# Five of seven Strassen products of the first two units as four-byte matmuls, and what moves with them

## The chip, the cores and the metric

One NeuronCore of a Trainium2 chip. The metric is the time of one execution on the device in microseconds (us). TensorE multiplies matrices, VectorE and ScalarE work element by element, GpSimd (POOL) does small things and issues the stores, SyncE (SP) issues the loads.

## The reference

A trunk of two layers, 2048 prompt tokens and 8 x 8 sample tokens, 1024 channels, all float32:

```python
h = rms_norm(x, pre_g)
z = jnp.einsum("btd,de->bte", h, w_in)          # 1024 -> 6 * 512
...
o = jnp.einsum("bte,ed->btd", jnp.concatenate([ya, yb], axis=-1), w_out)
return x + rms_norm(o, post_g), new_a, new_b
```

In the first layer (even) the mixers are a gated convolution of 3 taps (A) and a causal pooling with windows 2, 4, 8, 16 whose result goes through a 128 x 128 matrix per group (B). In the second (odd) they are a spatial gating within chunks of 128 tokens (C) and a convolution of 31 taps with a layer norm (D).

## The kernel before, in words

The work has six phases. Phases 0 and 1 are the input projection of layer 0 for the prompt's first and second 1024 tokens (a segment), phase 2 its output projection; phases 3 to 5 are the same for layer 1. A phase of input projection has 12 units. A unit multiplies 256 output channels by 1024 tokens, as one Strassen step in Winograd's form: seven products instead of eight, each of 4 tiles over the contraction (`KH` = 4), 128 x 128 by 128 x 512. Weights are the stationary side (A), activations the moving one (B). To reach float32 accuracy with matmuls in the reduced four-byte type `float32r`, each operand is split into a rounded high part (a cast on ScalarE) and a low part (a subtraction on VectorE), and each tile takes three matmuls: low by high, high by low, high by high (`mms`, L931 to L937). The activations' parts are `Bh` and `Bl`, split by `b_split` (L671); the weights' are `ahi` and `alo`, by `a_unit` (L477) and `lo_job` (L449). The sums of weight quarters (`comb`, L540) and of activation quarters (L829) that Strassen needs are made by VectorE too. Phase 0 writes its weights' sums and their low parts to DRAM (`wsd`, `wld`), and phase 1 loads them from there (L405 to L423).

The product order is `ORDER` (L44); for the first two units, which run as a pair, it is `FIRST` (L45). A pair (`TWINS`, L63) takes turns by product: unit 0's product j, unit 1's product j, so that what a product needs has twice the time. Pairs are units 0 and 1 and units 10 and 11 of phase 0, and units 10 and 11 of phase 3. The last unit of a phase frees one activation buffer after the other, and the next phase's activations are loaded (`b_proc`, L679) and split into them.

`start_proc` (L746) prepares phase 0. It loads the transposed prompt in two halves of 512 tokens, squares it (ScalarE) and adds the squares (VectorE, L762), sums over partitions with TensorE (L767), takes the mean and the root (L773 to L776), spreads the result over the partitions with four diagonal tiles `dg` and TensorE (L778 to L784), normalises 16 tiles in place (L744) and forms the sums. `h1_proc` (L837) does this for the second segment, stores the sums in DRAM (`td`, L702 to L709), and only then do the loads of phase 1's activations find all they need. `smp_states` (L1103) loads a state of the samples at the beginning of phase 1 and copies it with ScalarE. `pool_mix` (L1148) is mixer B's matrix. In the output projections, `unit_z` (L1066) leaves two PSUM banks per 128 tokens, and `post` (L1955) normalises them with VectorE, adds the residual and, in layer 0, transposes the result for phase 3.

The order of all instructions is found while the program is built, by a planner (`Plan`, L79): processes yield what they wait for (a condition, a time, VectorE time), and at each step of TensorE's planned time the first process that is ready goes on, in order of priority, 0 first. VectorE is filled at most 1 us ahead of TensorE. Each engine then runs its queue in that order. On-chip buffers are 36 slots shared by three classes, `U` (results), `Wp` (weights) and `R` (loads); `KEEP` (L34) reserves some per phase.

## Time and profile before

| | us |
|---|---|
| median of 3 runs | 1560.34 |
| lowest, highest | 1555.58, 1560.35 |
| the profiled execution | 1556.43 |
| its span, first to last instruction | 1554.7 |
| TensorE busy | 1479.5 (95%) |
| VectorE busy | 1100.3 (71%) |
| ScalarE busy | 768.1 (49%) |
| mean granted clock of TensorE | 0.981 |

The profile is of one execution. Matmuls are pipelined, so a matmul's recorded time is longer than the distance from its start to the next one's; the distance is its cost in a stream. A four-byte (unsplit) matmul is recorded as two instructions.

### The profile page before, as it was taken

How to read it: one execution, taken by the hardware profiler on the slowest of the kernel's cores; microseconds unless marked ns; L12 is line 12 of the kernel's file. 1: busy time of each engine (PE TensorE's matmuls, PEld its weight loads, DVE VectorE, ACT ScalarE, POOL GpSimd, SP SyncE). 2: the span in 40 equal slices, each digit the busy share in tenths (PEclk: the TensorE clock that was granted, in tenths of full speed). 3: DMA queues.
4: the chain of work that ended last, by engine and by line, in shares of the span. 5: the costliest groups of instructions: out<-in, count | busy, mean ns of one | idle time of the engine just before them, and what ended most of it. 6: DMA issues, size and time to landing. Idle time of an engine off the chain costs nothing. (4 is left out here: it accounts for less than half of the span.)

```text
span 1554.7 us, 22198 instructions
## 1 busy us (share of the span) xinstructions
PE 1479.5 (95%) x6762; PEld 1200.7 (77%) x6762; DVE 1100.3 (71%) x1853; ACT 768.1 (49%) x1606; POOL 439.9 (28%) x841
## 2 busy tenths in 40 slices
PE   5699999799999999999979999989999999899997
PEld 4588887688888888878857888868888878788775
DVE  6977787675656557667663798978578988885532
ACT  5555434464554454445455655555544455724411
POOL 1243433112121105665643311000120023234421
PEclk9799999999999999999989999989999999999999
DMA  4466777989788878899999899998557688947641
GB/s 171 161 214 228 276 251 272 318 271 329 267 315 271 281 235 264 288 308 345 346 359 347 272 323 355 331 337 273 176 164 220 196 264 275 306 153 224 200 147 61
DMA packets 230297, 403.92 MB, mean 260 GB/s; under 512 B 28450, under 2 KB 77874, under 8 KB 230179
## 3 DMA queue, kind: packets, MB, share of 16 engines
q1 hardware_dynamic: 190466, 274.09, 54.1%
q0 software_dynamic: 39712, 128.43, 22.0%
q8 instruction: 53, 0.87, 0.2%
q14 instruction: 66, 0.53, 0.1%
HBM read 272.96 MB, written 129.45 MB: 259 GB/s over the span
## 5 line engine op out<-in xcount | busy, mean ns | idle before, releaser
L935 PE MATMUL bank_b<-Bh,alo 128*128 128x512 f32 (+1 forms) x848 | 342.3, 404 | 21.8 <-DVE alo L452 11.3
L935 PE MATMUL bank_b<-Bl,ahi 128*128 128x512 f32 (+1 forms) x848 | 337.2, 398 | 4.0 <-ACT ahi L285 4.0
L935 PE MATMUL bank_b<-Bh,ahi 128*128 128x512 f32 (+1 forms) x848 | 336.5, 397 | 0.0
L285 ACT CAST ahi<-araw 128x512 fp32r<-128x512 f32 (+1 forms) x404 | 238.4, 617 | 23.0 <-DMA araw<-yd 6.1
L935 PE MATMUL bank_a<-Bh,alo 128*128 128x512 f32 (+1 forms) x496 | 202.0, 407 | 5.4 <-DVE o L1972 3.3
L935 PEld LDWEIGHTS bank_b<-Bh,alo 128*128 128x128 f32 (+1 forms) x848 | 160.2, 189 | 59.9 <-ACT ahi L285 9.9
L935 PE MATMUL bank_a<-Bl,ahi 128*128 128x512 f32 (+1 forms) x496 | 198.3, 400 | 6.0 <-ACT ahi L285 4.8
L935 PE MATMUL bank_c<-Bh,alo 128*128 128x512 f32 (+1 forms) x496 | 198.9, 401 | 2.1 <-ACT Bh L285 2.0
L935 PE MATMUL bank_c<-Bl,ahi 128*128 128x512 f32 (+1 forms) x496 | 196.8, 397 | 4.0 <-ACT ahi L285 2.8
L935 PE MATMUL bank_a<-Bh,ahi 128*128 128x512 f32 (+1 forms) x496 | 197.0, 397 | 0.0
L935 PE MATMUL bank_c<-Bh,ahi 128*128 128x512 f32 (+1 forms) x496 | 196.3, 396 | 0.0
L935 PEld LDWEIGHTS bank_b<-Bl,ahi 128*128 128x128 f32 (+1 forms) x848 | 160.5, 189 | 40.8 <-ACT ahi L285 4.9
L935 PEld LDWEIGHTS bank_b<-Bh,ahi 128*128 128x128 f32 (+1 forms) x848 | 160.2, 189 | 39.2
L452 DVE TENSOR_TENSOR alo<-araw,ahi 128x512 fp32r<-128x512 f32 (+1 forms) x164 | 108.3, 681 | 74.3 <-ACT ahi L285 72.7
L935 PEld LDWEIGHTS bank_a<-Bl,ahi 128*128 128x128 f32 (+1 forms) x496 | 94.2, 190 | 27.7 <-ACT ahi L285 6.2
L935 PEld LDWEIGHTS bank_a<-Bh,alo 128*128 128x128 f32 (+1 forms) x496 | 94.1, 190 | 25.8 <-DVE o L1972 3.7
L935 PEld LDWEIGHTS bank_c<-Bl,ahi 128*128 128x128 f32 (+1 forms) x496 | 93.5, 188 | 25.4 <-ACT ahi L285 4.0
L935 PEld LDWEIGHTS bank_a<-Bh,ahi 128*128 128x128 f32 (+1 forms) x496 | 93.9, 189 | 22.5
L935 PEld LDWEIGHTS bank_c<-Bh,alo 128*128 128x128 f32 (+1 forms) x496 | 93.2, 188 | 23.2 <-ACT Bh L285 2.4
L935 PEld LDWEIGHTS bank_c<-Bh,ahi 128*128 128x128 f32 (+1 forms) x496 | 93.3, 188 | 22.5
L1487 DVE SCALAR_TENSOR_TENSOR fc<-fs,wsum,fc 128x512 f32<-128x512 f32 x120 | 90.1, 751 | 3.4
L675 DVE TENSOR_TENSOR Bl<-braw,Bh 128x512 fp32r<-128x512 f32 x116 | 74.5, 686 | 24.9 <-ACT Bh L285 24.7
(283 smaller groups left out, 2426.1 us busy)
## 6 DMA issues: line engine op xcount, KB each, us to landing
araw<-wx SPq DMA_DIRECT2D x144, 256.0 KB
araw<-wsd SPq DMA_DIRECT2D x144, 256.0 KB
alo<-wld SPq DMA_DIRECT2D x144, 256.0 KB
alo<-wlx SPq DMA_DIRECT2D x96, 256.0 KB
praw<-wi SPq DMA_DIRECT2D x72, 256.0 KB
araw<-yd SPq DMA_DIRECT2D x64, 256.0 KB
araw<-wi SPq DMA_DIRECT2D x48, 256.0 KB
wld<-alo POOLq DMA_DIRECT2D x48, 256.0 KB, 3.8
```

What stands on the lines that cost most here:

```text
L285: nc.scalar.copy(out=out, in_=in_)
L452: nc.vector.tensor_tensor(out=lo, in0=x, in1=hi.bitcast(F32), op=SUB)
L675: nc.vector.tensor_tensor(out=Bl[j][:, k, :], in0=r, in1=Bh[j][:, k, :].bitcast(F32), op=SUB)
L935: nc.tensor.matmul(out=out[:m], lhsT=w[k][:, :m], rhs=r[:, k, :], start=(start and k == 0 and w is l), stop=(stop and k == KH - 1 and w is ...
L1487: nc.vector.scalar_tensor_tensor(out=C, in0=sm[:, j:j + HM], scalar=w, in1=C, op0=MUL, op1=ADD if j else SUB)
```

## The change

Units 0 and 1 of phase 0 compute products 0, 3, 1, 5, 2 (`PLAIN`, in that order) with unsplit operands, one four-byte matmul per tile (`mms_plain`), products 4 and 6 as before. `a_first` makes their weights, `start_proc` orders norms, sums and splits anew; all 28 activation tiles are still split, for the later units. Low parts of weight sums 1, 2 and 5 of these units are not stored; phase 1 makes them itself (`no_low`). Units 10 and 11 of phase 0 are no pair any more. `h1_proc` and the posts of `unit_z` go to priority 1. The last output unit of phase 2 copies its banks to slots. Mixer B's matrix takes one four-byte matmul in segment 0 and for the samples. The output states are stored later.

```diff
-KEEP = ((18, 14), (12, 16), (16, 10), (14, 12), (18, 10), (12, 10))
+KEEP = ((22, 10), (12, 16), (16, 10), (14, 12), (18, 10), (12, 10))
-FIRST = (0, 3, 1, 2, 4, 5, 6)
+FIRST = (0, 3, 1, 5, 2, 4, 6)
+
+PLAIN = (0, 3, 1, 5, 2)
-TWINS = ((0, 0), (0, 10), (3, 10))
+TWINS = ((0, 0), (3, 10))
...
+    def no_low(lay, i, j):
+
+        return lay == 0 and (j in XT or i < 2 and j in PLAIN)
...
-                        lo, _ = load(kind, wld[lay][i, SIDX[j]], "alo", F32R)
+                        lo = None if no_low(lay, i, j) else load(kind, wld[lay][i, SIDX[j]], "alo", F32R)[0]
...
-                               and (u > 1 or st["x"] >= 3) and (kind == "w" or y_tile_ready(lay, key, i)))
+                               and (u > 1 or st["x"] >= 3) and (u != 2 or (1, 2) in prod) and (kind == "w" or y_tile_ready(lay, key, i)))
...
+    def a_first(u):
...
+        def later(j, n=1):
+            yield ("c", lambda: (u, j) in prod)
+            Wp.free(n)
+        sat = {}
+        yield from fetch(0)
+        plain(0, x[0])
+        yield from fetch(3)
+        plain(3, x[3])
+        yield from fetch(1)
+        yield from fetch(2)
+        yield ("c", Wp.room)
+        S = Wp.take([P, 512], "asum")
+        yield from comb(1, S, x[1], x[2], ADD)
+        plain(1, S)
+        yield from comb(4, x[1], x[0], x[1], SUB)
+        yield ("c", lambda: (u, 0) in prod)
+        yield ("u", sat[1])
+        yield from comb(2, x[0], S, x[0], SUB)
+        plain(2, x[0])
+        pl.spawn(later(1), 2)
+        yield ("c", lambda: (u, 3) in prod)
+        yield from comb(5, x[3], x[3], x[0], SUB)
+        plain(5, x[3])
+        pl.spawn(later(2), 2)
+        pl.spawn(later(5), 2)
+        yield ("c", lambda: all((e, 1) in prod for e in range(2)))
+        yield from split(4, x[1], pl.dve)
+        yield from split(6, x[2], pl.pe)
...
-            at = act(out=s4, in_=ps, dep=pl.pe)
+            nc.vector.tensor_scalar(out=s4, in0=ps, scalar1=1.0 / DM, scalar2=EPS, op0=MUL, op1=ADD)
...
-                dg = sp.tile([P, P], F32, tag="dg", name="dg", bufs=2)
+                dg = dgs[:, i * P:(i + 1) * P]
...
-            pl.spawn(by_columns(c), 1)
+            pl.spawn(by_columns(c), 0)
...
+        yield ("c", lambda: len(prog[0]) == 4)
+        yield ("t", 0.3)
+        yield from norm(0, range(KD))
+        aux_free()
+        yield ("c", lambda: len(prog[1]) == 4)
+        yield ("t", 0.3)
+        for k in range(KH):
+            split(0, k, (0, k))
+        yield from norm(1, range(KH))
+        yield ("c", lambda: (0, 1) in made and (1, 1) in made)
+        yield ("c", both(0))
+        yield from sums(1, (0, 0), (1, 0), (0, 0), 0)
+        yield from norm(1, range(KH, KD))
+        aux_free()
+        yield ("c", lambda: (0, 5) in made and (1, 5) in made)
+        yield ("c", both(1))
+        yield from sums(2, (0, 0), (1, 1), (0, 0), 1)
+        yield from sums(4, (1, 0), (1, 1), (1, 0))
+        for k in range(KH):
+            pl.spawn(drop(4, k, lambda: True), 1)
+            split(3, k, (0, k + KH))
+        yield ("c", both(3))
+        yield from sums(6, (0, 1), (0, 1), (0, 0), 3)
+        for k in range(KH):
+            split(5, k, (1, k + KH))
...
+    def mms_plain(out, ph, u, j, start):
+        t, = a_need(u, j)
+        w = f4(t[0])
+        for k in range(KH):
+            if (j, k) not in plain_ok:
+                pl.drain(lambda: (j, k) in plain_ok)
+            nc.tensor.matmul(out=out, lhsT=w[:, k, :], rhs=plain_x[j, k], start=(start and k == 0), stop=(k == KH - 1),
+                             skip_group_check=True)
+            pl.tick(0.92)
+        del ready[u, j]
+        prod.add((u, j))
...
+            if u + 1 == phase_units[2][1]:
+
+                t = U.take([P, 512], "o")
+                act(out=t[:m], in_=bk[:m])
+                done_bank(key)
+                bk, key = t, None
...
-        pl.spawn(go(), 2)
+        pl.spawn(go(), 1)
...
+        if whole:
+            w = cst[:, C_PW + cb * P:C_PW + (cb + 1) * P]
+            nc.tensor.matmul(out=ps[:, :n], lhsT=w, rhs=dd, start=True, stop=True)
+            pl.pe += 0.92
...
-                yield from pool_mix(cb, dd[:, 0:CH], CH, self.sg[c], dd[:, 0:CH], dh, dl)
+                yield from pool_mix(cb, dd[:, 0:CH], CH, self.sg[c], dd[:, 0:CH], self.s == 0)
...
-        yield ("c", lambda: all(y_ready(0, b, NPR, NSAMP) for b in range(KD)) and U.room())
+        yield ("c", lambda: all(y_ready(0, b, NPR, NSAMP) and y_ready(0, b, SEG + CH, CH) for b in range(KD)) and U.room())
...
-        pl.spawn(h1_proc(), 3)
+        pl.spawn(h1_proc(), 1)
```

## Rows read from the trace of the kernel before

**Rows 1.** The page, busy us by engine, and TensorE's busy tenths in 40 slices.

```profile
PE 1479.5 (95%) x6762; PEld 1200.7 (77%) x6762; DVE 1100.3 (71%) x1853; ACT 768.1 (49%) x1606; POOL 439.9 (28%) x841
...
PE   5699999799999999999979999989999999899997
```

**Rows 2.** Busy us (instructions) in stretches; then PEclk, DMA share, GB/s.

```profile
20.00:27.20 7.20, 3.99 (x16) 3.62 (x17) 5.71 (x11) 3.07 (x8) 1.26 (x2) 1.00 0.01 2
27.20:63.40 36.20, 22.46 (x74) 16.07 (x73) 36.13 (x61) 19.29 (x35) 4.48 (x8) 0.83 0.12 44
63.40:88.20 24.80, 24.75 (x98) 19.99 (x99) 17.07 (x29) 12.52 (x23) 7.62 (x16) 0.90 0.79 276
88.20:236.00 147.80, 147.80 (x645) 119.82 (x644) 115.84 (x200) 70.32 (x150) 60.87 (x113) 1.00 0.71 246
```

**Rows 3.** Waits of TensorE: us in total, times, longest.

```profile
PE bank_b L935 <- DVE alo L452: 11.3, 2, 9.5
...
PE bank_b L935 <- ACT bank_b L285: 8.0, 1, 8.0
```

**Rows 4.** Timeline of TensorE in units 0 and 1: start, us, instruction.

```profile
27.24 0.77 PE L935 MATMUL bank_a<-Bh,alo 128*128 128x512 f32 x1
...
38.15 0.40 PE L935 MATMUL bank_a<-Bh,ahi 128*128 128x512 f32 x1
38.38 0.39 PE L935 MATMUL bank_a<-Bh,alo 128*128 128x512 f32 x1
...
46.79 0.63 PE L935 MATMUL bank_c<-Bh,alo 128*128 128x512 f32 x1
47.21 0.63 PE L935 MATMUL bank_c<-Bl,ahi 128*128 128x512 f32 x1
...
63.45 0.77 PE L935 MATMUL bank_b<-Bh,alo 128*128 128x512 f32 x1 [9.50 <-DVE alo L452]
...
88.34 0.40 PE L935 MATMUL bank_a<-Bh,alo 128*128 128x512 f32 x1
```

**Rows 5.** Groups of VectorE from 20 to 67 us: count, busy us, mean ns.

```profile
L675 DVE TENSOR_TENSOR Bl<-xT,Bh 128x512 fp32r<-128x512 f32 x24 | 14.9, 681 | 0.2 <-ACT Bh L285 0.2
L744 DVE SCALAR_TENSOR_TENSOR xT<-xT,cst,rb 128x512 f32<-128x512 f32 x16 | 11.0, 740 | 0.0
L829 DVE TENSOR_TENSOR xT<-xT 128x512 f32<-128x512 f32 x16 | 9.9, 680 | 0.0
```

**Rows 6.** Timeline of TensorE, the gating product in phase 3.

```profile
857.78 1.05 PE L1629 MATMUL sg<-wmb,v 128*128 128x128 f32 x8
```

**Rows 7.** Timeline of ScalarE and of VectorE at the start.

```profile
17.04 0.40 ACT L781 ACTIVATE dg<-ident,r 128x128 f32<-128x128 f32 x1 [1.20 <-PE rb L784]
...
21.60 0.74 DVE L744 SCALAR_TENSOR_TENSOR xT<-xT,cst,rb 128x512 f32<-128x512 f32 x1
```

**Rows 8.** Timeline of TensorE in units 10 and 11 of phase 0.

```profile
262.72 0.53 PE L935 MATMUL bank<-Bh,alo 128*128 128x512 f32 x1 [2.46 <-DVE alo L452]
```

**Rows 9.** Timeline of VectorE and of SyncE's queue before phase 1.

```profile
285.80 0.68 DVE L707 TENSOR_TENSOR xT<-xT,xT 128x512 f32<-128x512 f32 x1
...
290.13 0.32 SPq L691 DMA_DIRECT2D braw<-td  x1
```

**Rows 10.** Phase 1's first unit: timeline of ScalarE, then stretches as in rows 2.

```profile
306.29 0.75 ACT L285 COPY smp<-stmp 128x64 f32<-128x64 f32 x2 [7.37 <-DMA stmp<-sab]
...
309.01 0.57 ACT L285 COPY bank_b<-bank_a 128x512 f32<-128x512 f32 x1
...
301.60:309.60 8.00, 0.00 (x0) 0.00 (x0) 2.02 (x4) 3.31 (x8) 0.00 (x0) 0.65 1.05 389
309.60:315.00 5.40, 5.36 (x14) 4.26 (x15) 5.17 (x10) 3.84 (x8) 0.00 (x0) 0.57 0.76 262
```

**Rows 11.** Phase 2 to phase 3: timeline of TensorE, then the stretch.

```profile
791.76 0.80 PE L935 MATMUL bank_a<-Bh,alo 128*128 128x512 f32 x1 [3.31 <-DVE o L1972]
...
783.00:791.80 8.80, 2.52 (x11) 1.47 (x9) 7.76 (x13) 7.85 (x16) 7.03 (x8) 0.63 1.03 378
```

More of the change, by code (lines that the diff above doesn't have):

```diff
@@ L447, in trunk, with fetch, plain, comb @@
     made = set()
+    prod, plain_ok = set(), set()
+    def a_first(u):
+        i = seq[u][3]
+        x = {}
+        def fetch(q):
+            yield ("c", lambda: (u, q) in raws)
+            x[q], at = raws.pop((u, q))
+            yield ("u", at)
+        def plain(j, t):
+            ready[u, j] = (t,)
+            made.add((u, j))
+        def comb(j, out, p, q, op):
+            yield ("d", tt_cost(512))
+            nc.vector.tensor_tensor(out=out, in0=p, in1=q, op=op)
+            sat[j] = store(wsd[0][i, SIDX[j]], out, lambda: s_ok[0].add((i, j)))
+        def split(j, t, at):
+            yield ("c", lambda: Wp.room(2))
+            hi = Wp.take([P, 512], "ahi", F32R)
+            lo = Wp.take([P, 512], "alo", F32R)
+            at = act(out=hi, in_=t, dep=at)
+            def after():
+                if j in SIDX:
+                    store(wld[0][i, SIDX[j]], lo.bitcast(F32), lambda: l_ok[0].add((i, j)))
+                Wp.free()
+            pl.spawn(lo_job(t, hi, lo, at, (u, j), after), 0)
+        def later(j, n=1):
[26 more added lines that the diff above has]
+        yield from split(6, x[2], pl.pe)
     def lo_job(x, hi, lo, at, key, after):
@@ L786, in by_columns, with both, drop, have @@
             yield ("t", 1.2)
+            R.free()
             prog[c].extend(range(4))
         def split(j, kk, key):
-            pl.spawn(b_split(0, j, kk, x[key], pl.dve + 0.12, U.free if j in (4, 5, 6) else lambda: None), 1)
+            pl.spawn(b_split(0, j, kk, x[key], pl.dve + 0.12, lambda: None), 1)
+        def both(*js):
+            return lambda: all((e, j) in prod for e in range(2) for j in js)
+        def drop(j, kk, more):
+            yield ("c", lambda: (j, kk) in bready[0] and more())
+            U.free()
+        def have(j, kk, key):
+            plain_x[j, kk] = x[key]
+            plain_ok.add((j, kk))
         def columns(c):
@@ L818, in start_proc @@
             for k in range(KH):
                 def key(cq):
[L820 to L827 removed]
+                    return cq[0], cq[1] * KH + k
@@ L1019, in bank_take, with fin12 @@
                 take_bank(key[k])
+        def fin12():
+            bank_free("c")
+            con.c12_done()
         for j in combos(u):
-            hl = parts(u, j)
-            b_wait(ph, j)
+            plain = u < 2 and j in PLAIN
+            if not plain:
+                hl = parts(u, j)
+                b_wait(ph, j)
             if j in (0, 1):
@@ L1964, in post @@
         for h in range(2):
-            o.append(U.take([P, 512], "o"))
+            o.append(U.take([P, 512], "o") if banks[h][1] is not None else banks[h][0])
         gpost, gpre = rows["gpost"], rows.get("gpre")
```

109 lines of the change are left out of this document (56 added, 53 removed).

## The prediction, made before the run

> **What bounds the kernel now.** I read the page's busy line and 40 slices first. TensorE is busy for 1479.5 of 1554.7 us [rows 1], so at most 75 us of idle time can be won, plus what is lost at half clock. The slices say where: the first two, hardly any in the middle. Next I cut the start into stretches [rows 2]. From 27.2 to 63.4 us TensorE works 22.46 of 36.2 us, while VectorE is busy 36.13 of 36.2 us with 61 instructions, 0.59 us each: there **VectorE sets the pace**. From 88.2 to 236 us TensorE has no idle time at all, and VectorE 116 of 148. So what is won at the start must be won in units 0 and 1. The waits of TensorE [rows 3] name the rest: 11.3 us for a low part of the weights (9.5 of it in one wait) and 8.0 us for one copy of a bank, elsewhere.
>
> The timeline of TensorE [rows 4] gives prices. The pair of units begins at 27.24 us, unit 2 at 88.34: 61.1 us. Split matmuls of 512 columns stand 0.23 us apart at full clock (38.15, 38.38) and 0.42 to 0.43 at 1.2 GHz (46.79, 47.21). The pair has 2 x 7 x 4 x 3 = 168 of them, 39.0 us at 0.232; so 22 us go to waits and half clock. What VectorE does meanwhile [rows 5]: 24 low parts of the activations, 16 normalisations, 16 sums. The low parts stand ahead of the weights' sums in its queue: the matmul at 63.45 waited 9.50 us.
>
> **The change, part by part.**
>
> *Matmuls.* 2 x 5 x 4 = 40 groups of three split matmuls become one four-byte matmul each. The nearest row is the gating product: eight recorded instructions, four four-byte matmuls of 128 columns, 1.05 us from the first start to the last end [rows 6]. Each of the eight lasts some 0.27 us, so the starts stand (1.05 - 0.27) / 7 = 0.111 us apart, and 4 x 128 = 512 columns take 8 x 0.111 = 0.89 us. Three split ones take 0.70. So TensorE gets 40 x 0.19 = 7.7 us more work, and the pair needs 40 x 0.89 + 16 x 0.70 = 46.7 us. The bounds: 0.70 (no dearer) and 1.05 (the row whole); I take 0.89. The Trainium skill, page "FP8 and Floating Point Precision", section "TensorE Precision Notes", has true FP32 take four passes through the array. By that rule a matmul costs 4 x 0.23 = 0.93 us and the pair 48.3; the trace agrees within 5%.
>
> *The start.* Four diagonal tiles take a slot each in one buffer, where two took turns: ScalarE's second waited 1.20 us for TensorE [rows 7], and with it the squares of the second half. The mean is taken by VectorE straight from PSUM, no copy. I take 1 us per half. The first normalisation began at 21.60 us [rows 7], and a plain product needs nothing but that: first matmul at 22 us, not 27.24. If the planner leaves the second half's statistics ahead of it on TensorE, as now, it is 25.5.
>
> *The pair.* 22 + 46.7 + 2.5 (half clock: 0.90 of 24.8 us in the second stretch [rows 2], as one warm-up) + 3 (the statistics matmuls between; TensorE was busy 3.99 us with such from 20 to 27.2 [rows 2]) + 2 for stalls = **76**. Is VectorE in time? Until the fifth product's operands exist it must do 16 normalisations, 8 sums of activations, 8 of weights and 8 low parts: 40 x 0.6 = 24 us from 20.4, so 44.5, while TensorE comes to that product at 22 + 5.5 + 4 x 7.1 = 56. Products 4 and 6 need 24 more, the leftover splits 8 more and the banks' sums 6: 23 us, so 67, against 69 for product 6. Close; hence the 2 us. Gain: 88.3 - 76.2 = **12 us**, between 88.3 - 71.2 = 17 (no stall, no statistics between) and 88.3 - 84 = 4 (late first matmul, 6 us of stalls). The cover is VectorE's remaining queue: if it runs late, unit 2 waits instead, since its tiles are now fetched only after unit 1's product 2.
>
> *What is moved off.* Ten casts and ten subtractions fewer here, 10 x 0.6 = 6 us of VectorE (in the sum above already), and six stores of low parts on GpSimd's queue. Phase 1 loads six tiles fewer on SyncE's queue, but makes these six low parts itself: 3.6 us of VectorE where activations are being split too.
>
> *Twin (0, 10) gone, h1 at priority 1.* These go together. The pair cost a wait of 2.46 us at 262.72 [rows 8], and it was there to spread phase 1's 28 activation splits over two units. But the sums for phase 1 ended at 285.80 us, and SyncE issued the load that needs them at 290.13 [rows 9]: the splits could not spread anyway. With h1 earlier they can begin at unit 11, with 19.5 us for 28 x 0.6 = 16.8 us of VectorE; behind each wait there stand the low parts of unit 12's weights. I cost that at a new stall of 2.5 us against 2.5 saved: 0, bounds +4 and -6.
>
> *The copy of the samples' state.* Late loads filled the DMA queues (1.05 from 301.6 to 309.6 us), ScalarE stood 7.37 us before the copy of the state, behind it the bank's copy, and TensorE 8.0 us [rows 3, 10]; then 0.57 of the clock for 5.4 us costs 2.3 more [rows 10]. The wait on that DMA stays in the code; what goes is the crowd of loads ahead of it. I take 7 of 10.3, bounds 0 and 10.3.
>
> *Last output unit of phase 2.* Its banks are copied by ScalarE (two copies, 0.57 us each as the bank's copies) and freed; phase 3 waited 3.31 us for VectorE's reading of one, and TensorE worked 2.52 of 8.8 us there [rows 11], 6.3 idle, with 0.63 of the clock. ScalarE is at 7.85 of 8.8 us and the DMA at 1.03 there, so the next weights come late. I take 5, bounds 0 and 8.8. Posts at priority 1 go with this.
>
> *Pooling.* Eight products of the first segment whole: 8 x 0.19 = +1.5 us of TensorE; eight casts and subtractions less, hidden. The samples' four, the later state store and KEEP: 0, beside a busy TensorE; bounds +1 and -1.
>
> Sum: 12 + 0 + 7 + 5 - 1.5 = 22.5 us off the profiled execution's 1556.4 (span 1554.7): 1533.9. The median of the runs is 1560.34, 3.9 above; two of three lie there, one at 1555.58. I add half of that: **1536**.
>
> **The rivals.**
>
> *Only the pair pays.* A new plan puts new stalls at the boundaries for the old: for it, the DMA at 1.03 to 1.05 in both [rows 10, 11]. 12 - 1.5 = 10.5: 1546, so 1548 as a median. Chance 0.22.
>
> *The debt is paid in units 2 to 5.* VectorE has 32 us free of 148 there [rows 2], yet h1 at priority 1 goes ahead of the weights' low parts, and product splits are left over; 10 us of waits come where none are. 1557, chance 0.10.
>
> *Turns: slower.* The sums are written in place over tiles that plain matmuls read, so VectorE's queue waits for TensorE, and TensorE then for the 8 instructions behind: 4.8 us at three changes of product, 14.4, and 2.5 of half clock after each, 7.5. The pair would end at 98, 9.8 later than now, the pooling adds 1.5, and the boundaries, whose work hangs on that queue, stay: 1567.7, so 1570 as a median. Against it: product 3 lies between 0 and 1, and 5 between 1 and 2, 7.1 us of cover for 4.8. It decides if unit 2 starts after 88.3. Chance 0.09.
>
> *TensorE the bound.* If the waits of the pair were hidden, only dearer matmuls would be left: 7.7 + 1.5, so 1566 and 1568 as a median. For it speaks 95% busy, against it the 13.7 us idle of 36.2 [rows 2]. The four-pass rule above speaks for this. Chance 0.03.
>
> **How the numbers follow.** Forecast 0.56. A difference under 0.3%, 4.7 us, can't be told from none. Faster: 0.56 + 0.22 + 0.02 of the debt's case, 0.80; same 0.08; slower 0.09 + 0.03 = 0.12. Low end: 17 + 4 + 10.3 + 8.8 off 1556.4, 1516. High end: past the second case and the debt's, 1558. That leaves out the slower cases and little else. The forecast's own range is 1516 to 1546.
>
> **What would show it.** Right: plain matmuls, two recorded each, 0.89 us a pair of records, the first at 22 us, unit 2 at 74 to 78; phase 1 begins near 280 with no wait of 7 us before the state's copy; a product of phase 3 straight behind the last output unit. Wrong: VectorE idle before sums with TensorE as the releaser (turns), waits of units 2 to 5 for low parts (debt), or a full DMA and the same gaps at both boundaries.

## The result, and the profile after

The changed kernel takes **1544.38 us** (median of 5 runs, 1539.90 to 1547.83), the kernel before 1560.34 in the 5 runs beside them. The ratio is **0.9902, 95% interval 0.9872 to 0.9931**: faster by about 1%, some 16 us. The profiled execution took 1544.38 us, its span is 1542.7 us, so 12.0 shorter than the span of before that the prediction was summed against. The forecast had 22.5 there.

The page first: busy times by engine, then TensorE's busy tenths.

```profile
PE 1482.0 (96%) x6710; PEld 1186.9 (77%) x6710; DVE 1090.5 (71%) x1839; ACT 758.6 (49%) x1584; POOL 439.7 (29%) x833
...
PE   6999999999999999999989999988999999899997
```

Against [rows 1] TensorE's busy time hardly moved (the plain matmuls are dearer), its first slices filled (5 6 9 9 to 6 9 9 9 in short), and nothing of the middle tells where 10 us went missing. For that the two traces have to be laid side by side. The same instructions are looked up in both, and the difference of their starts is the gain so far. The samples' matmuls (`zs`, one group after product 0 and one after product 6 of each unit) mark phases 1 and 4; the squares of the posts (`junk`, 34 of them) mark phase 2.

```
                                    before   after    gain so far
unit 2, first matmul                  88.3     76.1      12.2
phase 1, group 1 of the samples      297.7    284.3      13.4
phase 1, group 2                     326.5    306.9      19.6
phase 1, group 4                     350.8    334.8      16.0
phase 2, first squares               579.8    563.5      16.3
phase 2, last squares                785.4    774.5      10.9
phase 3, first transpose (vt)        839.5    827.0      12.5
phase 4, group 25                   1060.8   1042.5      18.3
phase 4, group 26                   1079.5   1067.0      12.5
last split matmul                   1546.3   1534.4      11.9
```

Up to phase 2 the gain is 16.3 us, where the forecast's terms for that stretch (12 + 0 + 7 - 1.5) make 17.5. From there on the forecast added 5 more; the kernel lost 4.4. **So the first half of the forecast came nearly as worked out, and the second half is where it fell short.** Both traces are single executions, and what that means for the second half shows only in the experiments.

*The pair.* TensorE's timeline (start, us, instruction; two records are one four-byte matmul):

```profile
19.68 2.08 PE L1049 MATMUL bank_a<-xT,araw 128*128 128x512 f32 x2 [1.82 <-DVE xT L813]
...
23.11 5.47 PE L1049 MATMUL bank_a<-xT,araw 128*128 128x512 f32 x6
28.37 1.24 PE L857 MATMUL rb<-dgs,ones 128*128 128x128 f32 x8
...
32.88 3.60 PE L1049 MATMUL bank_a<-xT,araw 128*128 128x512 f32 x8
36.32 3.60 PE L1049 MATMUL bank<-xT,araw 128*128 128x512 f32 x8
...
67.73 0.50 PE L1039 MATMUL bank_b<-Bl,ahi 128*128 128x512 f32 x1 [1.40 <-DVE Bl L744]
...
69.92 0.79 PE L1039 MATMUL bank_b<-Bl,ahi 128*128 128x512 f32 x1 [1.23 <-DVE Bl L744]
...
76.11 0.40 PE L1039 MATMUL bank_a<-Bh,alo 128*128 128x512 f32 x1
```

The first plain matmul starts at 19.68, unit 2 at 76.11 ([rows 4]: 27.24 and 88.34). Four matmuls start 36.32 - 32.88 = 3.44 us before the next four: 0.86 each. The wait of 9.50 us is gone; in its place stand two short ones in product 6, both for VectorE's low parts of the activations. The same stretch by engines (busy us and instructions of TensorE, weight loads, VectorE, ScalarE, GpSimd; PEclk, DMA share, GB/s):

```profile
19.60:28.80 9.20, 9.12 (x19) 4.99 (x20) 5.78 (x12) 0.88 (x3) 1.80 (x2) 0.50 0.04 15
28.80:66.00 37.20, 37.20 (x104) 18.76 (x103) 34.42 (x57) 20.52 (x39) 4.87 (x9) 1.00 0.42 136
66.00:76.10 10.10, 7.47 (x25) 5.43 (x24) 9.60 (x17) 5.73 (x10) 0.54 (x1) 0.83 0.24 86
76.10:224.00 147.90, 145.77 (x626) 116.04 (x625) 113.67 (x195) 67.92 (x148) 64.91 (x119) 1.00 0.73 256
```

From 28.8 to 66 us TensorE has no gap; VectorE works 34.42 of 37.2 us beside it. Before, it was the other way round [rows 2]. The last line is new against [rows 2] too: units 2 and on, where TensorE had no idle time, now have 2.1 us of it.

*The rest.* TensorE's waits, us in total, times, longest:

```profile
PE bank_c L1039 <- ACT ahi L287: 10.2, 5, 4.8
...
PE bank_a L1039 <- ACT ahi L287: 5.9, 4, 3.0
PE bank_b L1039 <- ACT ahi L287: 5.8, 3, 3.0
...
PE bank_b L1039 <- DVE Bl L744: 2.6, 2, 1.4
PE tp L2151 <- ACT junk L289: 2.5, 1, 2.5
...
PE pm L1299 <- DVE pw L1262: 1.8, 1, 1.8
```

Of [rows 3] the 9.5 for a low part and the 8.0 for a copied bank are gone. Waits for high parts of weights (`ahi`) grew from 11.9 us over all banks to 22.2, at the beginnings of phases 3 and 4 above all. ScalarE's timeline at the beginning of phases 1 and 4, two stretches:

```profile
283.50 0.76 ACT L287 COPY smp<-stmp 128x64 f32<-128x64 f32 x2
...
1044.73 1.23 ACT L287 COPY smp<-stmp 128x480 f32<-128x480 f32 x2 [4.28 <-DMA stmp<-sd]
```

In phase 1 the copy of the samples' state has no idle time worth a mark ahead of it ([rows 10]: 7.37). In phase 4 the sister of that copy, which the prediction never looked at, stands 4.28 us for its load; before it was 0.35:

```profile
1059.12 1.20 ACT L285 COPY smp<-stmp 128x480 f32<-128x480 f32 x2 [0.35 <-DMA stmp<-sd]
```

TensorE then stands 4.81 us for a high part that ScalarE has queued behind that copy, and is granted 0.50 of the clock, 1.2 GHz, until 1052.7 us (timeline of TensorE in the changed kernel: phase 1's pooling, the end of phase 2, the beginning of phases 3 and 4):

```profile
318.54 0.47 PE L1299 MATMUL pm<-dp,pw 128*128 128x512 f32 x1 [1.83 <-DVE pw L1262]
...
738.66 1.04 PE L2151 MATMUL tp<-ident,xres 128*128 128x128 f32 x4 [2.54 <-ACT junk L289]
...
780.35 0.80 PE L1039 MATMUL bank_c<-Bl,ahi 128*128 128x512 f32 x1 [2.51 <-ACT ahi L287]
...
787.64 0.50 PE L1039 MATMUL bank_b<-Bl,ahi 128*128 128x512 f32 x1 [1.80 <-ACT ahi L287]
...
1048.62 0.80 PE L1039 MATMUL bank_c<-Bl,ahi 128*128 128x512 f32 x1 [4.81 <-ACT ahi L287]
```

The lines at 318, 738 and 1048 us stand where the table of gains steps down; the two at 780 and 788 stand in the stretch behind phase 2, where it rises by 1.6. The experiments ask which of them belong to an edit.

### The profile page after: what moved, and what is told of

It is laid out like the page before. It is cut to its first block, busy times and chain, and to the rows that moved or that the text cites. A ratio compares the mean times of both kernels' runs of the same rounds, so it can differ in the third digit from the quotient of the medians.

```text
span 1542.7 us, 21993 instructions
## 1 busy us (share of the span) xinstructions
PE 1482.0 (96%) x6710; PEld 1186.9 (77%) x6710; DVE 1090.5 (71%) x1839; ACT 758.6 (49%) x1584; POOL 439.7 (29%) x833
## 3 DMA queue, kind: packets, MB, share of 16 engines
q0 software_dynamic: 39232, 126.86, 21.8%
## 4 chain that ended last, share of the span: by engine, by line
PE 74%; DMA 8%; issue 7%; DVE 4%; POOL 3%; ACT 3%; SPq 0%; POOLq 0%; ACTq 0%; DVEq 0%
PE bank_b L1039 30%; PE bank_c L1039 18%; PE bank_a L1039 17%; PE zs L1062 1%; PE zs L1063 1%; DMA hd<-xres 1%; DMA araw<-wx 1%; PE sg L1767 1%; DMA xres<-xp 1%; DVE Bl L744 1%; ACT Bh L287 1%; PE bank_a L1049 1%; ACT ahi L287 1%; PE bank L1049 1%; DMA braw<-td 1%
## 5 line engine op out<-in xcount | busy, mean ns | idle before, releaser
L1039 PE MATMUL bank_b<-Bl,ahi 128*128 128x512 f32 (+1 forms) x840 | 333.8, 397 | 8.5 <-ACT ahi L287 5.8
L1039 PE MATMUL bank_b<-Bh,alo 128*128 128x512 f32 (+1 forms) x840 | 338.6, 403 | 2.9 <-DVE alo L520 2.9
L1039 PE MATMUL bank_b<-Bh,ahi 128*128 128x512 f32 (+1 forms) x840 | 332.1, 395 | 0.0
L287 ACT CAST ahi<-araw 128x512 fp32r<-128x512 f32 x400 | 235.6, 618 | 21.3 <-DMA araw<-yd 7.1
L1039 PEld LDWEIGHTS bank_a<-Bh,alo 128*128 128x128 f32 (+1 forms) x496 | 93.2, 188 | 22.2 <-ACT sig L289 2.4
L1604 DVE SCALAR_TENSOR_TENSOR fa<-glu,cst,fa 128x513 f32<-128x513 f32 x120 | 89.9, 749 | 0.0
```

The costliest lines, as they stand in the source:

```text
L287: nc.scalar.copy(out=out, in_=in_)
L1039: nc.tensor.matmul(out=out[:m], lhsT=w[k][:, :m], rhs=r[:, k, :], start=(start and k == 0 and w is l), stop=(stop and k == KH - 1 and w is ...
L1604: nc.vector.scalar_tensor_tensor(out=A[:, 0:HM + 1], in0=ev[:, j:j + HM + 1], scalar=w, in1=A[:, 0:HM + 1], op0=MUL, op1=ADD)
```

## The experiments

Diffs are against the changed kernel unless a sentence says otherwise. The gains so far are read as in the table above, against the same profiled execution of before.

### The start alone, and all but the start

The first kernel keeps the plain products with their own order (`a_first`, `start_proc`, `KEEP`) and takes the other parts back:

```diff
-TWINS = ((0, 0), (3, 10))
+TWINS = ((0, 0), (0, 10), (3, 10))
...
-            if u + 1 == phase_units[2][1]:
+            if False:
...
-        pl.spawn(go(), 1)
+        pl.spawn(go(), 2)
...
-                yield from pool_mix(cb, dd[:, 0:CH], CH, self.sg[c], dd[:, 0:CH], self.s == 0)
+                yield from pool_mix(cb, dd[:, 0:CH], CH, self.sg[c], dd[:, 0:CH], False)
...
-        pl.spawn(h1_proc(), 1)
+        pl.spawn(h1_proc(), 3)
```

> The change with everything outside the start undone: the pair (0, 10) is back, h1 at priority 3, the posts at 2, no copy of the last output unit's banks, mixer B's matrix split as before, the states stored as before. Theory (the pair's gain is its own and stays): unit 2 starts at 75 to 77 us as in the changed kernel, against 88.3 before, the waits at 262 and before the copy of the samples' state return, and the whole is 8 to 12 us under the kernel before. Rival (the debt of the pair is paid later): unit 2 starts as early, but phase 1 begins less than 4 us earlier than before, and the whole is within 5 us of before.

The second is the kernel before with these parts alone (diff against before):

```diff
-TWINS = ((0, 0), (0, 10), (3, 10))
+TWINS = ((0, 0), (3, 10))
...
+            if u + 1 == phase_units[2][1]:
+                t = U.take([P, 512], "o")
+                act(out=t[:m], in_=bk[:m])
+                done_bank(key)
+                bk, key = t, None
...
-        pl.spawn(go(), 2)
+        pl.spawn(go(), 1)
...
-        pl.spawn(h1_proc(), 3)
+        pl.spawn(h1_proc(), 1)
```

> The kernel before with everything of the change but the start: units 0 and 1 stay split. Theory (the rest pays where it was put, and loses elsewhere): unit 2 at 88 us as before; the 8 us wait before the copy of the samples' state goes or falls under 2 us, some 7 us won by the second unit of phase 1; the whole is 0 to 6 us under before, since phase 2 loses with posts at priority 1. Rival (the boundary gains hang on the earlier pair): the wait of 8 us stays, and the whole is within 2 us of before.

Measured: the start alone 1549.23 us (1546.84 to 1554.95, 10 runs), ratio **0.9948 (0.9928 to 0.9968)**; the rest alone 1550.78 (1547.75 to 1555.79, 10 runs), **0.9950 (0.9934 to 0.9967)**. The two add up to -1.02%, the whole change is -0.98%. Each half is worth some 8 us; of the rest alone at most 6 had been expected.

For the start that is less than its 11.2 at unit 2, and its trace says where the rest goes. It has the pair's gain early in unit 2, but some 120 split matmuls later, at 117.3 us of before, the gain is 4.7. That is the debt that the prediction gave a chance of 0.10: VectorE comes out of the pair with work left over, and TensorE waits for it (the start alone):

```profile
85.10 0.50 PE L1039 MATMUL bank_b<-Bh,alo 128*128 128x512 f32 x1 [1.13 <-DVE alo L520]
...
98.39 0.49 PE L809 MATMUL rb<-dg,ones 128*128 128x128 f32 x2 [1.12 <-DVE dg L807]
```

The whole change pays 3.3 there (12.2 to 8.9), and every version with the plain start in the runs below pays between 3.3 and 5. (The trace of the start alone is of the longest of its ten executions, 1554.95 us.)

The start alone also keeps the waits that the other parts were meant to take away. TensorE at the pair of units 10 and 11 and in phase 1's first unit, then ScalarE before it:

```profile
257.00 0.79 PE L1039 MATMUL bank<-Bh,alo 128*128 128x512 f32 x1 [2.92 <-DVE alo L520]
...
303.37 0.77 PE L1039 MATMUL bank_b<-Bh,alo 128*128 128x512 f32 x1 [7.63 <-ACT Bh L287]
```

```profile
298.39 0.75 ACT L287 COPY smp<-stmp 128x64 f32<-128x64 f32 x2 [5.91 <-DMA stmp<-sab]
```

And the rest alone keeps the pair's (TensorE), but not the state's wait (ScalarE):

```profile
64.04 0.77 PE L935 MATMUL bank_b<-Bh,alo 128*128 128x512 f32 x1 [9.38 <-DVE alo L452]
```

```profile
298.65 0.76 ACT L285 COPY smp<-stmp 128x64 f32<-128x64 f32 x2
```

So the wait of [rows 10] is not tied to the start. It goes with `h1_proc` and the pair, as the prediction had it; the runs on these two follow below.

### What sets the pace of the pair

Each plain product does only its last contraction tile, ten matmuls of 40, at the same planned cost:

```diff
-            nc.tensor.matmul(out=out, lhsT=w[:, k, :], rhs=plain_x[j, k], start=(start and k == 0), stop=(k == KH - 1),
-                             skip_group_check=True)
+            if k == KH - 1:
+                nc.tensor.matmul(out=out, lhsT=w[:, k, :], rhs=plain_x[j, k], start=start, stop=True,
+                                 skip_group_check=True)
```

> The changed kernel where each plain product of units 0 and 1 does one of its four contraction tiles (the last), 10 matmuls instead of 40; three quarters of these products are left out; the planned cost and so the order of the other engines is as it was. TensorE is asked for 25.8 us less there. Theory (in the changed kernel TensorE sets the pace of the pair until product 4, and VectorE again from there, so what TensorE saves is little): unit 2 starts at 64 to 72 us, 4 to 12 earlier than 76.1, since VectorE needs about 45 us for all it does between the first normalisation and product 6. Rival (TensorE alone sets the pair's length, the dearer matmuls are paid in full): unit 2 starts before 56 us, 20 us or more earlier.

TensorE loses 30 x 0.86 = 25.8 us of work, and unit 2 starts at 70.4 us in place of 76.1: **5.7 earlier**. The rest went into waits, the two longest for VectorE, the third for ScalarE's copy of a bank, which stands in its queue behind casts of VectorE's sums (timeline of TensorE):

```profile
36.15 2.08 PE L1050 MATMUL bank_c<-xT,asum 128*128 128x512 f32 x2 [7.39 <-DVE xT L905]
...
44.42 2.04 PE L1050 MATMUL bank<-xT,araw 128*128 128x512 f32 x2 [3.55 <-DVE araw L473]
...
53.55 0.77 PE L1039 MATMUL bank_b<-Bh,alo 128*128 128x512 f32 x1 [3.13 <-ACT pb L287]
```

and the stretches show it as plainly:

```profile
20.00:70.40 50.40, 32.90 (x82) 19.24 (x82) 49.50 (x84) 27.39 (x50) 7.22 (x12) 0.80 0.36 118
```

VectorE works 49.5 of 50.4 us. The changed kernel is within 6 us of what VectorE needs for this stretch in this order: both engines now bound the pair almost alike, and a still cheaper matmul would bring no more than that. (One execution, 1535.2 us; nothing hangs on its total.)

### The pair of units 10 and 11, and the second segment's preparation

Two kernels, one edit each:

```diff
-        pl.spawn(h1_proc(), 1)
+        pl.spawn(h1_proc(), 3)
```

> The changed kernel with the preparation of the second segment at priority 3 again. Theory (the earlier sums are what lets phase 1's splits begin during unit 11): the sums for phase 1 end after 270 us, TensorE waits 5 us or more in phase 1's first two units, the whole is 3 to 8 us over the changed kernel. Rival (without the pair 10 and 11 they end early anyway): they end before 250 us, and the whole is within 2 us of the changed kernel.

```diff
-TWINS = ((0, 0), (3, 10))
+TWINS = ((0, 0), (0, 10), (3, 10))
```

> The changed kernel with units 10 and 11 of phase 0 as a pair again, the second segment's preparation at priority 1. Theory (pair and late sums go together; with early sums the pair spreads the splits but costs its own wait): a wait of 2 to 3 us in the pair comes back, with 1.6 us of half clock, the wait of 2.2 us at phase 1's first product goes, the whole is within 3 us of the changed kernel. Rival (the pair itself made the late loads and the 8 us wait before the state's copy): a wait of 5 us or more stands in phase 1's first unit, the whole is 5 to 10 us over the changed kernel.

With `h1_proc` back at priority 3 its last store is issued at 282.42 us (241.91 in the changed kernel, 286.78 before), and half of the wait of [rows 10] is back. ScalarE, then TensorE:

```profile
289.94 0.75 ACT L287 COPY smp<-stmp 128x64 f32<-128x64 f32 x2 [4.03 <-DMA stmp<-sab]
```

```profile
293.30 0.80 PE L1039 MATMUL bank_b<-Bh,alo 128*128 128x512 f32 x1 [3.64 <-ACT bank_b L287]
```

With the pair back and `h1_proc` at 1 that wait stays away, but the pair itself stalls (TensorE):

```profile
266.16 0.80 PE L1039 MATMUL bank_c<-Bh,alo 128*128 128x512 f32 x1 [6.13 <-DVE alo L520]
```

Group 2 of phase 1 comes at 312.3 and 312.8 us in the two, against 306.9: each edit is worth 5 to 6 us *there*, and the start alone, without both, reaches it at 320.1, 13.2 later (some 3 of these are its larger debt). The totals say something else: 1542.08 us (0.9885, 0.9852 to 0.9918) and 1539.03 (0.9856, 0.9830 to 0.9882), neither slower than the change itself, though the late preparation had been expected to cost 3 to 8 us and the pair's wait to be 2 to 3. What they lost in phase 1 they did not lose again in phase 2. So the mechanism is shown at its place; what it is worth in the total isn't.

### The last output unit of phase 2, and the posts

```diff
-            if u + 1 == phase_units[2][1]:
+            if False:
```

> The changed kernel without the copy of the last output unit's banks (the posts stay at priority 1). Theory (the copy frees the bank for phase 3 and is worth what the wait for VectorE's reading cost): TensorE waits 3 us or more for VectorE's reading of a bank at the end of phase 2 again, phase 3's first chunk comes 3 to 6 us later after phase 2's end, the whole 2 to 6 us over the changed kernel. Rival (the full DMA holds phase 3's weights back, whichever bank is free): the first chunk comes within 1.5 us of the changed kernel's place, the whole within 2 us.

```diff
-        pl.spawn(go(), 1)
+        pl.spawn(go(), 2)
```

> The changed kernel with the posts of the output units at priority 2 again. Theory (priority 1 puts the posts' squares on ScalarE ahead of the next unit's square and makes the waits before transposes at 673 and 735 us): the waits of 1.4 and 2.5 us before transposes go, phase 2 is 3 to 6 us shorter, the boundary to phase 3 is 0 to 3 us worse, the whole 0 to 5 us under the changed kernel. Rival (the waits come from stores that land late while the DMA is full): the same waits for VectorE or ScalarE before transposes stay, the whole is within 2 us of the changed kernel or slower.

Without the copy the wait of [rows 11] is back (2.36 us for VectorE's reading), and the waits for weights behind it get shorter (4.6 us in three up to the first transpose, with the copy 7.2 in five); TensorE:

```profile
773.70 0.67 PE L1039 MATMUL bank_a<-Bh,alo 128*128 128x512 f32 x1 [2.36 <-DVE o L2110]
...
789.25 0.50 PE L1039 MATMUL bank_c<-Bl,ahi 128*128 128x512 f32 x1 [2.69 <-ACT ahi L287]
```

From the last squares to phase 3's first transpose it is 52.9 us, 52.5 with the copy, 54.1 before. The copy had been expected to be worth 3 to 6; the rival, that phase 3 comes within 1.5 us of its place, holds. ScalarE makes the copy ahead of the last squares and so moves that mark by 0.6 us: the 0.4 us are no gain. The three stretches by engines, before, changed kernel, without the copy:

```profile
785.40:839.50 54.10, 47.36 (x191) 37.30 (x192) 21.97 (x34) 25.32 (x50) 20.48 (x28) 0.87 0.97 358
```

```profile
774.50:827.00 52.50, 45.27 (x188) 34.92 (x188) 21.75 (x34) 26.80 (x53) 16.41 (x27) 0.93 1.02 383
```

```profile
769.50:822.40 52.90, 45.26 (x190) 35.25 (x191) 22.26 (x34) 26.53 (x53) 17.25 (x28) 0.97 1.03 385
```

The DMA share is 0.97 to 1.03 in all three, and GB/s times us is 19.4, 20.1 and 20.4 MB: transfers go on all through it. Freeing the banks 2 to 3 us earlier only moves TensorE's wait from the bank to the next weights. That the full DMA makes these late is argued, not shown: in the two versions below whose boundary is 7 us shorter than before the share is 1.04 and 1.03 too, at 18.3 and 18.2 MB. Nor does one pair of runs settle what the copy is worth in another order: over the table below the three versions without it take 52.9 to 54.1 us, the eleven with it 46.8 to 53.1. The total without the copy, 1549.52 us (0.9931, 0.9906 to 0.9956), is 5 us higher by the median, but its profiled execution, the fastest of its six, has a span of 1542.2, the changed kernel's 1542.7, and no stage of it is longer for a reason that the copy could have; it is left open.

With the posts at priority 2 the wait of 2.54 us at 738.66 is gone and one of 2.13 at 677.00 is left (1.36 in the change); phase 2, first to last squares, takes 209.1 us in place of 211.0, the total is 1540.78 (0.9888, 0.9853 to 0.9924). Expected were both waits gone and a phase 2 shorter by 3 to 6 us. The 1.9 us are inside what executions of one order differ by, as the last experiment shows.

### The state of phase 4, and the pooling's matrix

The state's loads leave their place at the phase's beginning and are issued a unit earlier (two units in phase 3); the copy stays where it is:

```diff
+    def smp_load(lay):
+        ts = []
+        for src in (a["sab"],) if lay == 0 else (a["sd"][:, 0:480], a["sd"][:, 480:960]):
+            t = U.take([P, src.shape[1]], "stmp")
+            nc.sync.dma_start(out=t, in_=src)
+            pl.moved(src.shape[1])
+            ts.append(t)
+        smv["in", lay] = ts
...
+            if ph + 1 in SAMPLE_PH and u == phase_units[ph][1] - (2 if ph == 3 else 1):
+                smp_load((ph + 1) // 3)
```

> The changed kernel with the loads of the samples' states issued one unit earlier (two units in phase 3), the copies where they are. Theory (phase 4 lost 4.8 us and half clock after it because ScalarE stands before the state's copy, with the weights' casts behind it): ScalarE's wait of 4.3 us at 1044 us goes, the 4.8 us wait of TensorE falls under 1.5, and the whole is 4 to 8 us under the changed kernel. Rival (the DMA queues are full there, the weights come late anyway): another wait of 3 us or more stands at the same place, and the whole is within 2 us of the changed kernel.

Measured: **1535.09 us (1532.05 to 1539.07), ratio 0.9847 (0.9810 to 0.9884)**. ScalarE and TensorE at the beginning of phase 4:

```profile
1038.85 1.10 ACT L287 COPY smp<-stmp 128x480 f32<-128x480 f32 x2
```

```profile
1042.59 0.67 PE L1039 MATMUL bank_c<-Bl,ahi 128*128 128x512 f32 x1 [0.30 <-ACT ahi L287]
```

The wait of 4.81 us is 0.30, and groups 25 to 26 take 19.4 us in place of 24.5: 5.1 us, the wait and the 1.2 GHz behind it. How much of that is the edit's depends on what it is held against. The kernel with the price 0.86 (below) has the changed kernel's order and late loads, waits 1.89 us before the copy and takes 21.8 us for these groups, so there it would be 2.4; with the pair of units 10 and 11 back they take 19.9 without the early loads and 19.4 with them. The other 4 us by which its median lies under the change's have no cause in the edit's mechanism. Its profiled execution, the longest of its four, is 5.4 us shorter than the changed kernel's, and 3.8 us of that come in phase 2 and at its end (259.7 us from the first squares to phase 3's transpose, 263.5 in the changed kernel), where the state has no part.

This edit with the pair of units 10 and 11 back, and this edit with the pooling's matrix split at unit 9 in place of just before its use:

```diff
+            if u == 9:
+                pw_tile()
```

> The changed kernel with the early load of the samples' states and units 10 and 11 as a pair. Theory (the state's copy is a wait of its own, whatever the order around it): ScalarE's wait before it in phase 4 is under 0.5 us, TensorE's 4.8 us at phase 4's first product goes, and the whole is 1 to 6 us under the changed kernel with the pair alone (1539). Rival (each new order finds another stall of the same size): the whole is 1537 or more.

> The changed kernel with the early load of the states, and mixer B's weights split in unit 9 of phase 0, not at their first use in phase 1. Theory (the wait of 1.8 us for that split at 318 us and 1.6 us of half clock after it are the new cost of the whole product in segment 0, which put the split off to phase 1): that wait goes, phase 1 is 2 to 4 us shorter, the whole 0 to 4 us under the kernel with the early state alone (1535). Rival (VectorE is behind there anyway): a wait of over 1 us for mixer B's operands stays at the same place.

The former: 1536.78 us (0.9870, 0.9846 to 0.9894); the state's copy of phase 4 waits for nothing, the pair stalls 6.13 us again, and group 26 comes at 1058.6 us against 1059.4 without the pair. The latter: 1542.32 us (0.9893, 0.9872 to 0.9914). Its first matmul on the matrix waits no longer, and groups 2 to 4 of phase 1 take 24.3 us (27.9 in the changed kernel, 25.9 with the early state, 24.3 before), so the wait of 1.83 us and the 1.2 GHz behind it are taken back. (With the pair back the same wait is 0.81 us, and the groups take 24.5.) The total is 7 us above the early state alone, where 0 to 4 below had been expected: 700 us later it has a wait that no other version has. TensorE, VectorE and ScalarE in phase 3's last unit:

```profile
1036.28 0.80 PE L1039 MATMUL bank_b<-Bh,alo 128*128 128x512 f32 x1 [9.46 <-ACT s L287]
```

```profile
1021.19 11.78 DVE L1630 SCALAR_TENSOR_TENSOR fc<-fs,wsum,fc 128x512 f32<-128x512 f32 x15
1033.01 0.88 DVE L1634 SCALAR_TENSOR_TENSOR glu<-fs,wsum,fc 128x256 f32<-128x256 f32 x2
```

```profile
1034.52 1.23 ACT L289 ACTIVATE sgd<-sgd 128x512 f32<-128x512 f32 x2 [13.11 <-DVE sgd L1094]
1035.66 0.57 ACT L287 COPY s<-bank_b 128x512 f32<-128x512 f32 x1
```

Fifteen taps of mixer D's convolution stand in one row on VectorE, ahead of a sum that ScalarE needs; ScalarE has the copy that frees `bank_b` queued behind that, and TensorE stands 9.46 us. In the version without the edit the same row stands ahead of the same sum, but begins at 1015.75 in place of 1021.19, and TensorE waits 2.43 us for the copy. Nothing of the matrix is near. Laid side by side, the two traces have one order there on every engine but VectorE, which in this version has eight other taps in a row just ahead of them, in the other version two. So an early edit has changed a late order, for the worse.

### The planner's price alone

If an early edit can deal the order of a late phase anew, an edit that changes no instruction may do so too. Only the planner's price of a plain matmul, 40 of which end by 61 us, goes from 0.92 to the measured 0.86:

```diff
-            pl.tick(0.92)
+            pl.tick(0.86)
```

> The changed kernel with nothing but the planner's price of a plain matmul at 0.86 us, as measured, and not 0.92: no operation is added or left out, only the order found may differ. Theory (phases 2 to 4 depend on the order that the planner happens to find, by as much as the forecast was off): unit 2 starts within 2 us of 76.1, yet the time from phase 2's first product to phase 3's first chunk differs by 2 us or more from the changed kernel's 263.5, and the whole by up to 6 either way. Rival (what phases 2 to 4 lost is fixed by the parts of the change): both within 1.5 us of the changed kernel.

Measured: 1536.95 us (1535.55 to 1546.10), ratio 0.9874 (0.9842 to 0.9907). The gain so far is 12.8 us at group 1 of phase 1 (13.4 in the changed kernel), 17.5 at phase 2's first squares (16.3) and **17.5 at its last (10.9)**. TensorE waits nowhere longer than 0.2 us for `junk`, the state of phase 4 waits 1.89 us in place of 4.28. Phase 2 and the boundary take 257.3 us, where a difference of 2 or more from 263.5 had been expected, so the theory seems borne out. Its reason isn't. **Laid side by side, the two traces have the same instructions in the same order from 61 us on**, on all five engines, but for two pairs of neighbours on VectorE at 76 and 242 us. The price changed the order of the start alone; the 5.4 us of phase 2 come with no change of order. Where 2.3 of them come about can be followed: TensorE's transposes come behind VectorE, and VectorE waits for the landing of a store (`td<-xres`). TensorE with the price 0.86, then VectorE in the changed kernel and with the price 0.86:

```profile
732.38 0.63 PE L2151 MATMUL tp<-ident,xres 128*128 128x128 f32 x4 [0.18 <-ACT junk L289]
```

```profile
732.58 1.42 DVE L2089 TENSOR_TENSOR xres<-xres 128x512 f32<-128x512 f32 x2 [2.65 <-DMA td<-xres]
```

```profile
726.29 1.42 DVE L2089 TENSOR_TENSOR xres<-xres 128x512 f32<-128x512 f32 x2 [1.80 <-DMA td<-xres]
```

From VectorE's instruction to the transposes it is 6.1 us in both. The price 0.86 lies 3.9 us ahead of the changed kernel at TensorE's matmul before, 6.3 at the transposes. Of these 2.3 the longer wait for the store makes 0.85; with the rest VectorE was already late.

With the early load of the state on top:

> The changed kernel with both edits that had gained by themselves: the loads of the samples' state issued a unit earlier (1535.09, 0.9847) and the planner's price of a plain matmul at 0.86 in place of 0.92 (1536.95, 0.9874, against 0.9902 of the change). Theory (the price has no worth of its own, it only deals the order of the work anew, and the order falls better or worse by some 7 us): the two don't add up. The wait before the state's copy of phase 4 stays under 1 us and its first stretch (second to third group of gates) near 19.5 us, since that belongs to the earlier load; phase 2 and the boundary behind it, from the first post to phase 3, come out somewhere from 252 to 265 us, as in all versions; the total 1530 to 1542, ratio 0.982 to 0.990. Rival (the measured price makes the plan right, so its 7 us come on top of the load's 9): 1528, ratio 0.980 or below.

1537.48 us (1534.85 to 1537.90), ratio 0.9873 (0.9852 to 0.9895). The state's copy of phase 4 waits for nothing and groups 25 to 26 take 19.2 us; phase 2 and the boundary take 256.4 us. But the start came out 3 us worse (a gain of 9.2 early in unit 2), and the two improvements don't add up: the rival, at 0.980, is out. From 61 us on its order is that of the early load alone, yet phase 2 takes 204.3 us against 209.8.

First to last squares of phase 2 and the boundary behind it, over all versions, in us:

```
                          phase 2    boundary
before                     205.6       54.1
the change                 211.0       52.5
start alone                211.3       53.5
rest alone                 206.6       46.8
state early                209.8       49.9
a quarter                  208.3       51.8
posts at 2                 209.1       50.7
h1 at 3                    205.4       47.2
pair 10, 11 back           205.0       50.7
no copy                    209.3       52.9
state early, pair back     204.9       51.6
state early, pw early      208.2       53.1
price 0.86                 205.6       51.7
state early, price 0.86    204.3       52.1
```

No part of the change separates the high rows from the low ones in the first column: the posts are at 1 in the change and in the last row alike, the copy is in both, `h1_proc` too. The order doesn't either. Over phase 2 five versions have one order on all engines: the change, a quarter, the price 0.86, "state early, pw early" and, up to its last unit, "no copy". They take 211.0, 208.3, 205.6, 208.2 and 209.3 us. Four others share a second order: "state early", "pair 10, 11 back", "state early, pair back" and "state early, price 0.86", with 209.8, 205.0, 204.9 and 204.3. So either order spreads over some 5.5 us, nearly as far as the whole column. The change, "no copy" and "posts at 2" are even one program up to the first squares, and their gains there are 16.3, 19.6 and 14.3 us. That is the variation of one kernel from run to run (1539.90 to 1547.83 for the change), seen in its traces, and a difference of 5 us in a late phase of one trace against one other shows nothing about an edit. Whether a changed start sets the late timing by way of its transfers, in the same order, stays open.

## Why the prediction was right, and where its sum was not

The sign, and that the gain would begin in the pair, were right. The time came out 8 us above the forecast, inside its range; the kernel with the price 0.86, whose order is the same from 61 us on, has a ratio of 0.9874 against 0.9902, so part of the 8 us may be what sets of runs differ by. By its steps:

- **The matmul, 0.89 us.** It is 0.86, nearer the gating product's estimate than either bound. The Trainium skill ("FP8 and Floating Point Precision", section "TensorE Precision Notes") has true FP32 take four passes. By four starts of a split matmul that made an estimate of 0.93; measured are 3.7 such starts, and the measurement decides. On 40 matmuls that is 2.8 us.
- **The first matmul at 22, unit 2 at 76.2, gain 12.** 19.7, 76.1 and 12.2. Of the parts, the first matmul was 2.3 us early and the matmuls 1.2 cheaper (40 x 0.03), the half clock dearer: 2.5 was allowed, and a granted 0.50 up to 28.8 us cost four plain matmuls 0.86 each, 3.4, and the warm-up after the two waits some 1.7 more. The stalls are 1.40 + 1.23 = 2.6 where 2 were allowed, at the very product 6 that the deadline sum (67 against 69) had called close. So the exact hit is partly luck: errors of 2 to 3 us cancel.
- **The debt, a rival at 10 us and 0.10.** It is there, but small: 3.3 us in units 2 to 4 (2.1 of it idle TensorE). It should have been a term of the sum rather than a case against it, since VectorE's leftover work was worked out in the prediction.
- **Twin gone and h1 earlier, 0, and the state's copy, 7.** Together the gain so far goes from 8.9 to 19.6 us at group 2 of phase 1, 10.7 where 7 was forecast. The runs don't let the two terms be parted, since each edit alone leaves one of the waits: 6.13 us with the pair, 4.03 with the late preparation. Costing the pair's end at 0 was too careful.
- **Pooling, -1.5.** -3.6 from group 2 to group 4 of phase 1. The wait of 1.83 us for the split matrix, which segment 0 no longer needs and phase 1 now makes at its first use, and the half clock behind it were not foreseen. The matrix split earlier gave all of it back, so the dearer products themselves cost nothing that is seen there; the wait is no fixed price either, 0.81 us with the pair back.
- **The copy of the last output unit, 5.** This is **the step that failed**, with the reason that stood beside it: "ScalarE is at 7.85 of 8.8 us and the DMA at 1.03 there, so the next weights come late". The boundary became 1.6 us shorter, without the copy it is 1.2 shorter. It was read as a wait for a bank; with the bank free TensorE waited for the next weights instead, 7.2 us in five waits, and the bank had only come last. Two versions (46.8, 47.2) did have a boundary 7 us shorter; what let them isn't known.
- **Nothing for phases 2 to 4 else.** The sum took them as they were, "beside a busy TensorE". They took 5.4 us in phase 2 and 5.8 at the beginning of phase 4, and gave 5.8 in phase 3. The state's wait of phase 4 is the one cause among these that an edit shows (2.4 to 5.1 us back). The 5.4 us of phase 2 belong to no part of the change: the price 0.86 takes 205.6 us in the same order, and one order spreads over 5.5. So here the sum missed nothing that is shown; it was held against one execution.

In one sum: 12.2 - 3.3 + 10.7 - 3.6 + 0.3 = 16.3 up to phase 2, then -5.4 + 1.6 + 5.8 - 5.8 - 0.6 = -4.4, so 11.9 (the span has 12.0). The rival "only the pair pays" gave 1548 as a median and lies nearer to 1544 than the forecast does, but for the wrong reason: the boundary of phase 1 did pay, and in this execution as much was lost again later. "Turns" didn't come: unit 2 starts 12 us before the point from which it would decide. "TensorE the bound" holds for the 37 us from 28.8 on, and no longer.

The lowest ratio is that of the change with the state's loads issued earlier: 1535.09 us, 0.9847 (0.9810 to 0.9884), the change's is 0.9902 (0.9872 to 0.9931). It isn't shown to be the better kernel: the version with its order from 61 us on and the price 0.86 has 0.9873, and 0.5 to 5.1 us at one place are all that its edit accounts for.

## What to carry to other kernels

Where one engine's deadline makes another wait, look for the work that needs no preparation: a dearer matmul (0.86 in place of 0.70 us) paid here because it needs none of the splits that VectorE was late with, and a run with a quarter of the matmuls showed how much there was left to win, 6 us. Before a wait at a boundary is put down to a bank, look at what is due next: here, with the DMA share at 1.0, the wait for the bank went and waits for weights came in its place. And before a difference in a late phase is put down to an edit or to a planner's order, lay the two traces' orders side by side: a phase of 205 us differed by 5 in the same order, while a changed order, where there was one, showed as a wait of 9.46 us with the queue that made it.

## What had not been expected

The pace of the first matmuls is not the program's alone. The changed kernel's profile has 0.50 from 8 to 28.8 us, and six records of plain matmuls take 5.47 us there; the version without the copy is the same program up to the end of phase 2, and takes 4.24 for the same six:

```profile
23.48 4.24 PE L1049 MATMUL bank_a<-xT,araw 128*128 128x512 f32 x6
```

Its records start 0.85 us apart up to 26.18 us, as the changed kernel's do, and 0.43 apart from 26.70 on. So its clock rose at about 26.4 us, the changed kernel's at 28.8, with the same instructions. Its gain early in unit 2 is 14.5 us, the change's 12.2: some 2 us of the pair's gain differ between executions.

The column of the granted clock misleads at this place. It shows 1.00 in the version without the copy from the first microsecond on, since that trace has no record of the clock before the rise at 26.35, and a stretch without a record is shown as 1.00. The version with the early state and the price 0.86 shows 1.00 from 19.6 to 28.8 us too, and its six records take 5.47; its first record is a rise at 29.94. The kernel before is such a trace as well: the 1.00 of [rows 2] up to 27.2 us is no measurement, and the split matmuls at 27.81, 28.24 and 28.66 us start 0.42 to 0.43 apart, those from 31.15 on 0.23. So half the clock at the start is no cost of the change; the kernel before began its pair with it too. A four-byte matmul of 512 columns in a stream, two records, starts 0.86 us before the next at 2.4 GHz and about 1.7 at 1.2 GHz (0.85 a record, from 24.11 to 28.37 us in the changed kernel): it scales with the clock like the split ones.
